# Natural key order in the sample's dilated mixture, and prompt heads prepared one head in front

## Chip, cores and metric

The kernel runs on one core of a Trainium2 chip. The metric is the device time of one execution in microseconds (us).

## What is computed

One hybrid encoder layer runs on two request groups with shared weights, a prompt of 512 tokens and a sample of 1024. Each group goes through an input layer norm, a token mixer, cross-attention into 256 memory tokens and a squared-ReLU MLP, with a layer norm behind each. The token mixer has eight heads of mixture a and eight of mixture b, 64 wide. Mixture a adds up three banded attentions, each with its own softmax, weighted by their log-sum-exp; b is a two-dimensional neighbourhood attention. What matters here is the pattern of a:

```
DILATED_PATTERNS = ((128, 1), (512, 4), (2048, 16))
def dilated_window_attention(q, k, v, window, dilation):
    # Query t attends to keys t + dilation*j, |j| <= (window/2)/dilation
    ...
    s = jnp.einsum('bdnqhc,bdnkhc->bdnhqk', qb, kb) * (hd ** -0.5)
    s = jnp.where(valid, s, NEG_INF)
    p = jnp.exp(s - m)
```

## The kernel before

All products are made from fp32r operands that are split in a high and a low part. A head's queries lie as one stack of 64 rows high and 64 rows low (qs), its keys as two stacks, k1 (high over low) and k2 (low over high), so that a score block is two matmuls, qs with k1 and qs with k2 (L502, L503).

Prompt heads of mixture a use one dense block of 512 keys per 128 queries. For the sample the three patterns are done in two kinds of units, four units a head. Units 1 and 2 (`attn_a1`, L579, first loop) are the local pattern: for each block of 128 queries, the up to 256 keys around it. Units 3 and 4 (second loop) are the dilated patterns: the tokens are split in four residue classes modulo 4, and each class of 256 queries meets its class of 256 keys, two blocks of 128 queries per class. A unit holds four blocks, so a head makes 16 score matmuls of each kind. The values of the dilated units are made by transposing every fourth column (L457); those of the local units by transposing adjacent columns (L409).

Before the change, the sample's keys lie in residue order over all 1024 tokens: all tokens of class 0, then 1, 2 and 3. For this, `stack` (L352) first copies 512 projected and rotated tokens, high part on ACT (L359) and low part on GpSimd (L360), into a buffer pair in residue order. The pair is `env["perm"]`, taken once from the tag "gb" (L650), so all 16 stacks of the sample use the same one. Eight DMAs on SP's queue (L366 to L370) then lay out the head: two natural query halves from the projection's buffers (hd<-qt) and six from the copies (hd<-gb), the residue queries and both key stacks, each row in four runs of 128 columns. A dilated unit then reads one run of keys, and a local unit reads four runs; its scores come out in residue order, and the masked maximum (L482) reads the mask and writes the probabilities with a step of four, so that the probabilities are natural again.

A head's attention (`unit`, L470) is a generator of four steps: scores, mask, maximum and exponentials; transposes of the probabilities and their split; products with v; transposing back. `push` (L566) adds a unit and lets each unit in flight take its next step; then it runs one entry of the mixer's `fill` list, if any. The plan holds 16 prompt heads and then 16 sample heads, a before b, in pairs that share weights and values; each has its preparation (weights, projections, `stack`, values, bias) and its units (one for a prompt head; four and two for sample heads of a and b). `attend` (L710) walks through them and spreads the preparation of later heads over the pushes of the present one. `lead(j)` says beside which head the preparation of head j stands: prompt heads stand two in front, sample heads one. Before that walk, head 0, the input norm of sample tile 8, head 1 and the input norms of tiles 9 to 11 are traced (L924). An input norm (`ln_in`, L220) loads 128 tokens, normalises them on VectorE, ACT and GpSimd (`layer_norm`, L148), stores them and transposes them eight times. Its gain and bias take two of the eight buffers of the tag "tok". A pair of prompt heads takes four of these eight: three for queries and keys, one for values.

The traced order is a priority: a scheduler takes what is ready by its own clock and gives out buffers as they come free, so engines need not follow the order of the source.

Of the kernel before, what the change touches and what calls it, by code (L numbers as in the profile page):

```python
# [31 lines left out]
def f32(ap):  # L32
    return ap.bitcast(F32)
# [3 lines left out]
def tile_encoder_layer(ctx: ExitStack, tc: tile.TileContext, d, outs):  # L37
# [232 lines left out]
    def mixer(r, fill):  # L270
# [80 lines left out]

        def stack(hd, sh, sl, g):  # L352

            qs, k1, k2 = hd[0:3]
            tt = slice(g * 512, (g + 1) * 512)
            kh, kl = sh, sl
            if r:
                kh, kl = env["perm"]
                A.activation(residues(kh), by_residue(f32(sh)), AF.Copy)  # L359
                G.tensor_copy(residues(kl), by_residue(f32(sl)))  # L360
                kh, kl = residues(kh), residues(kl)
                k1, k2, qp = (residues(k)[:, :, g * P:(g + 1) * P] for k in hd[1:4])
            else:
                k1, k2 = k1[:, tt], k2[:, tt]
            for o, x, y, z in ((slice(0, 64), sh, kh, kl), (slice(64, P), sl, kl, kh)):
                S.dma_start(f32(qs[o, tt]), f32(x[0:P:2]))  # L366
                if r:
                    S.dma_start(f32(qp[o]), f32(y[0:P:2]))
                S.dma_start(f32(k1[o]), f32(y[1:P:2]))
                S.dma_start(f32(k2[o]), f32(z[1:P:2]))  # L370

        def head_tile(is_b):
            t = act.tile([P, 4096], F32R, name="hd", tag="act")
# [93 lines left out]
                last = vt  # L467
                yield

        def unit(hd, v, h, blocks, norm=None, then=None, scale=1.0, local=False):  # L470

            qs, k1, k2 = hd[0:3]
            order, keyed = (by_residue, residues) if local else (lambda a: a, lambda a: a)
            st = sb.tile([P, 16], F32, name="st", bufs=4)
            probs, todo = [], []
            s, sx, pr, x = None, 512, None, 512

            def soften():  # L480
                for i, so, p, bias in todo:
                    V.tensor_tensor_reduce(out=order(p), in0=keyed(so), in1=order(bias), scale=1.0, scalar=LOWEST, op0=ALU.add,  # L482
                                           op1=ALU.max, accum_out=st[:, 8 + i:9 + i])
                    nm, den = st[:, 2 * i + 1:2 * i + 2], st[:, 2 * i:2 * i + 1]
                    V.tensor_scalar(nm, st[:, 8 + i:9 + i], -scale, None, op0=ALU.mult)  # L485
                    A.activation(p, p, AF.Exp, bias=nm, scale=scale, accum_out=den)  # L486
                todo.clear()
# [91 lines left out]
        def attn_a1(hd, v, h, tab, hg):  # L579
            for j in range(2):  # L580
                bl = []
                for b in range(4 * j, 4 * j + 4):
                    lead, n = (64, 192) if b == 0 else (0, 192) if b == 7 else (0, 256)
                    k0 = (b * P - 64 + lead) // 4
                    bl.append((cols(b * P, P), lambda z, k0=k0, n=n: residues(z)[:, :, k0:k0 + n // 4],
                               tab[:, lead:lead + n], n, lead, 256, (b, (b + 1) % 8)))

                def then(raw, j=j):
                    S.dma_start(oas[0][j * 512:(j + 1) * 512, hg].rearrange("(i p) c -> p i c", p=P), raw)
                push(unit(hd, v, h, bl, then=then, local=True))  # L590
                yield
            for j in range(2):
                bl = []
                for q in (2 * j, 2 * j + 1):
                    for i in range(2):
                        bl.append((cols(q * 256 + i * P, P), cols(q * 256, 256),
                                   tab[:, 384 - P * i:640 - P * i], 256, 0, 256, (8 + 2 * q, 9 + 2 * q)))

                def then(raw, j=j):
                    for i in range(2):  # L600
                        S.dma_start(oas[1].rearrange("(h p q) g c -> q p h g c", p=P, q=4)[2 * j + i, :, :, hg],
                                    raw[:, 2 * i:2 * i + 2])
                push(unit((hd[3],) + hd[1:3], v, h, bl, then=then))
                yield
# [102 lines left out]

        return [x for is_b in (False, True) for pair in range(4) for x in pair_ab(pair, is_b)]

    def attend(heads, lead, after=()):  # L710

        for k, (_, units, n) in enumerate(heads):
            work = [f for j in range(len(heads)) if lead(j) == k for f in heads[j][0]]
            if k == len(heads) - 1:
                work += after
            us, done = units(), 0
            for i in range(n):
                next(us)
                while done < len(work) * (i + 1) // n:
                    work[done]()  # L720
                    done += 1
            for _ in us:
                pass
# [9 lines left out]
    def merge(t):  # L733
# [15 lines left out]
        for i in range(2):  # L749
# [2 lines left out]
        V.tensor_add(o, o, t[1][:, :, 0:64])  # L752
        S.dma_start(os_[1][rows, 0:512].rearrange("p (g c) -> p g c", g=8), o)

    plan = mixer(0, []) + mixer(1, [None] * 36 + [call(merge, t) for t in range(8)] +
                                [call(tok_load, 0, t) for t in range(4)])


# [162 lines left out]
            for f in extra.get((h, 1), ()):  # L921
                f()

    for f in plan[0][0] + [call(ln_in, 8)] + plan[1][0] + [call(ln_in, i) for i in range(9, 12)]:  # L924
        f()
    attend(plan, lambda j: j - 2 if j < 16 else j - 1, [call(y_tile, 0, t) for t in range(4)])
    while pipe:
        step()
    w_out_half(0, 0)
# [348 lines left out]
```

## Time and profile before

| | us |
|---|---|
| median of 3 runs (lowest, highest) | 2386.12 (2379.81, 2386.31) |
| the profiled execution | 2380.81 |
| its span, first to last instruction | 2379.0 |
| TensorE matmul busy | 2284.5 |
| VectorE busy | 1608.6 |
| ScalarE (ACT) busy | 1022.7 |
| GpSimd (POOL) busy | 879.3 |

The profile is of one execution. PE is TensorE's matmuls, PEld its weight loads, which overlap them; DVE is VectorE; SP issues DMAs. A name such as hd<-gb says what is written and what is read; L-numbers are lines of the kernel. A wait row says which instruction stood idle and what it was released by.

### The profile page before, as it was taken

What the parts mean: (1) busy time and instruction counts of PE and PEld (TensorE: products, weight loads), DVE (VectorE), ACT (ScalarE), POOL (GpSimd) and SP (SyncE); (2) the same over time, 40 slices, a digit from 0 to 9 for tenths busy, and PEclk for the clock granted to TensorE, in tenths of its full rate; (3) what the DMA queues carried; (4) which work ended last, traced back from release to release, by engine and by line L of the source; (5) the groups of instructions that cost most, each with busy time, mean ns of one, the idle gap of its engine ahead of it and who ended that gap; (6) DMA issues with size and microseconds to landing.
All of it is one profiled execution on the core that took longest, in us unless ns stands there. A gap on an engine that the chain in (4) does not pass through costs nothing. (4 is left out here: it accounts for less than half of the span.)

```text
span 2379.0 us, 33108 instructions
## 1 busy us (share of the span) xinstructions
PE 2284.5 (96%) x11124; PEld 1892.7 (80%) x11124; DVE 1608.6 (68%) x3297; ACT 1022.7 (43%) x2176; POOL 879.3 (37%) x820
## 2 busy tenths in 40 slices
PE   8989998999999999999999999999999999999997
PEld 6868777888888787777878877878888888887875
DVE  6265635677656667668676487767776696689786
ACT  4345645666555532334333333333354322344541
POOL 7564443223324211433154355555541314310221
PEclk9999999999999999999999999999999999999998
DMA  9675345677535642435335444344489999974781
GB/s 318 201 228 146 78 117 121 137 137 150 116 95 135 180 124 92 133 115 176 117 107 185 121 155 147 120 139 147 149 223 221 210 222 250 224 177 156 165 206 68
DMA packets 410235, 375.21 MB, mean 158 GB/s; under 512 B 72513, under 2 KB 326481, under 8 KB 410065
## 3 DMA queue, kind: packets, MB, share of 16 engines
q1 hardware_dynamic: 367056, 339.54, 49.7%
q0 software_dynamic: 43008, 33.56, 10.1%
q8 instruction: 88, 1.44, 0.3%
q14 instruction: 83, 0.67, 0.1%
HBM read 290.76 MB, written 52.98 MB: 144 GB/s over the span
## 5 line engine op out<-in xcount | busy, mean ns | idle before, releaser
L107 POOL TENSOR_TENSOR wl<-wraw,wh 128x512 fp32r<-128x512 f32 x80 | 106.2, 1344 | 218.5 <-ACT wh L106 169.3
L1062 ACT ACTIVATE wh<-q 128x512 fp32r<-128x512 f32 x176 | 110.1, 626 | 140.5 <-DMA q<-in_w_up_dram 61.5
L486 ACT ACTIVATE q<-q,st 128x256 f32<-128x256 f32 (+3 forms) x256 | 138.4, 544 | 60.3 <-DVE st L485 59.0
L1063 DVE TENSOR_TENSOR wh<-q,wh 128x512 fp32r<-128x512 f32 x176 | 125.8, 717 | 54.2 <-ACT wh L1062 53.9
L321 POOL TENSOR_TENSOR wl<-wraw,wh 128x256 fp32r<-128x256 f32 x128 | 94.0, 757 | 160.3 <-ACT wh L320 144.9
L1047 POOL DMA_DIRECT2D q<-in_w_up_dram x64 | 83.3, 1416 | 181.0 <-DVE h L1100 72.8
L532 DVE TENSOR_TENSOR pt<-t,pt 128x512 fp32r<-128x512 f32 x160 | 105.2, 670 | 54.8 <-ACT pt L531 54.0
L1047 POOL DMA_DIRECT2D q<-in_w_down_dram x64 | 56.4, 921 | 218.9 <-DVE wraw L1134 92.9
L1000 POOL TENSOR_TENSOR wl<-pt,wh 128x512 fp32r<-128x512 f32 x64 | 91.6, 1451 | 118.6 <-ACT wh L999 118.4
L544 PE MATMUL o<-pt,tok 128*128 128x256 f32 (+3 forms) x576 | 116.1, 315 | 9.1 <-ACT q L550 8.6
L531 ACT ACTIVATE pt<-t 128x512 fp32r<-128x512 f32 x160 | 89.6, 579 | 80.1 <-PE o L544 76.4
L107 POOL TENSOR_TENSOR wl<-qt,wh 128x512 fp32r<-128x512 f32 x64 | 101.6, 1608 | 51.3 <-ACT wh L106 43.4
L1013 DVE TENSOR_TENSOR tok<-tok,t 128x512 f32<-128x512 f32 x124 | 82.9, 680 | 37.5 <-PE t L131 37.4
L1013 DVE TENSOR_TENSOR tok<-tok,s 128x512 f32<-128x512 f32 x124 | 83.8, 679 | 29.7 <-PE s L131 29.4
L131 PE MATMUL pj<-x20h,wl 128*128 128x512 f32 x256 | 101.4, 396 | 2.5 <-POOL wl L107 2.3
L119 POOL TENSOR_TENSOR wl<-wraw,wh 128x512 fp32r<-128x512 f32 x48 | 64.7, 1366 | 103.7 <-ACT wh L118 103.7
L129 PE MATMUL pj<-x20h,wh 128*128 128x512 f32 x256 | 100.6, 393 | 1.0 <-ACT wh L106 0.9
L528 PE MATMUL t<-ident,q 128*128 128x128 f32 x624 | 97.9, 276 | 3.3 <-ACT q L486 1.8
L158 POOL TENSOR_TENSOR lnst<-lnst,mhalf 128x1 f32<-128x1 f32 x44 | 54.2, 1234 | 124.7 <-DVE lnst L157 124.6
L130 PE MATMUL pj<-x20l,wh 128*128 128x512 f32 x256 | 100.2, 391 | 0.0
L544 PEld LDWEIGHTS o<-pt,tok 128*128 128x128 f32 x576 | 85.0, 192 | 16.5 <-ACT q L550 11.3
L999 ACT ACTIVATE wh<-pt 128x512 fp32r<-128x512 f32 x64 | 36.9, 624 | 121.7 <-PE s L131 103.2
(497 smaller groups left out, 7527.9 us busy)
## 6 DMA issues: line engine op xcount, KB each, us to landing
q<-in_w_up_dram SPq DMA_DIRECT2D x128, 256.0 KB
q<-in_w_down_dram SPq DMA_DIRECT2D x128, 256.0 KB
wraw<-in_w_in_dram SPq DMA_DIRECT2D x96, 256.0 KB
qt<-in_w_up_dram SPq DMA_DIRECT2D x32, 512.0 KB
pt<-in_w_down_dram SPq DMA_DIRECT2D x32, 512.0 KB
q<-in_w_up_dram POOLq DMA_DIRECT2D x64, 256.0 KB, 8.1
q<-in_w_down_dram POOLq DMA_DIRECT2D x64, 256.0 KB, 5.9
sa<-kv SPq DMA_DIRECT2D x28, 512.0 KB
```

The lines of the kernel that those rows point to most:

```text
L107: G.tensor_sub(wl[:, sl], r, f32(wh[:, sl]))
L129: T.matmul(out, lh[k], rh[k], start=(k == 0), stop=False, skip_group_check=True)
L130: T.matmul(out, lh[k], rl[k], start=False, stop=False, skip_group_check=True)
L131: T.matmul(out, ll[k], rh[k], start=False, stop=(k == n - 1), skip_group_check=True)
L486: A.activation(p, p, AF.Exp, bias=nm, scale=scale, accum_out=den)
L528: T.transpose(t[:, x:x + P], p, ident)
L532: V.tensor_sub(lo[:, 0:x], t[:, 0:x], f32(hi[:, 0:x]))
L544: T.matmul(o[:, q0:q0 + n], v(c, h), part[:, x:x + n], start=(done == 0 and part is hi), stop=(done == total - 1 and part is lo), skip_gro ...
L1013: V.tensor_add(x, x, q)
L1047: G.dma_start(out, src, accum_op=ADD)
L1062: A.activation(dst[0], x, AF.Copy)
L1063: low.tensor_sub(dst[1], x, f32(dst[0]))
```

## The change

In `stack` the keys go to their places in natural order, straight from the projection's buffers; only the queries for the dilated units come from the residue copy, in residue order within each 512 tokens. The local units read plain runs, and the masked maximum has no reordering any more. The dilated units take their queries from `512 * i + q * 128` and their keys as every fourth column. `lead` goes: every head is prepared one head in front, and the input norms of sample tiles 8 to 11 move into the prompt's `fill` list, beside its heads 1 to 4.

```diff
         def stack(hd, sh, sl, g):
             qs, k1, k2 = hd[0:3]
             tt = slice(g * 512, (g + 1) * 512)
-            kh, kl = sh, sl
+            ph, pl = env["perm"] or (None, None)
             if r:
-                kh, kl = env["perm"]
-                A.activation(residues(kh), by_residue(f32(sh)), AF.Copy)
-                G.tensor_copy(residues(kl), by_residue(f32(sl)))
-                kh, kl = residues(kh), residues(kl)
-                k1, k2, qp = (residues(k)[:, :, g * P:(g + 1) * P] for k in hd[1:4])
-            else:
-                k1, k2 = k1[:, tt], k2[:, tt]
-            for o, x, y, z in ((slice(0, 64), sh, kh, kl), (slice(64, P), sl, kl, kh)):
+                A.activation(residues(ph), by_residue(f32(sh)), AF.Copy)
+                G.tensor_copy(residues(pl), by_residue(f32(sl)))
+            for o, x, w, y in ((slice(0, 64), sh, sl, ph), (slice(64, P), sl, sh, pl)):
                 S.dma_start(f32(qs[o, tt]), f32(x[0:P:2]))
+                S.dma_start(f32(k1[o, tt]), f32(x[1:P:2]))
+                S.dma_start(f32(k2[o, tt]), f32(w[1:P:2]))
                 if r:
-                    S.dma_start(f32(qp[o]), f32(y[0:P:2]))
-                S.dma_start(f32(k1[o]), f32(y[1:P:2]))
-                S.dma_start(f32(k2[o]), f32(z[1:P:2]))
+                    S.dma_start(f32(hd[3][o, tt]), f32(y[0:P:2]))
...
-        def unit(hd, v, h, blocks, norm=None, then=None, scale=1.0, local=False):
+        def unit(hd, v, h, blocks, norm=None, then=None, scale=1.0):
...
-            order, keyed = (by_residue, residues) if local else (lambda a: a, lambda a: a)
...
-                    V.tensor_tensor_reduce(out=order(p), in0=keyed(so), in1=order(bias), scale=1.0, scalar=LOWEST, op0=ALU.add,
+                    V.tensor_tensor_reduce(out=p, in0=so, in1=bias, scale=1.0, scalar=LOWEST, op0=ALU.add,
...
-                    k0 = (b * P - 64 + lead) // 4
-                    bl.append((cols(b * P, P), lambda z, k0=k0, n=n: residues(z)[:, :, k0:k0 + n // 4],
-                               tab[:, lead:lead + n], n, lead, 256, (b, (b + 1) % 8)))
+                    bl.append((cols(b * P, P), cols(b * P - 64 + lead, n), tab[:, lead:lead + n], n, lead, 256,
+                               (b, (b + 1) % 8)))
...
-                push(unit(hd, v, h, bl, then=then, local=True))
+                push(unit(hd, v, h, bl, then=then))
...
-                        bl.append((cols(q * 256 + i * P, P), cols(q * 256, 256),
+                        bl.append((cols(512 * i + q * P, P), cols(q, 256, 4),
...
-    def attend(heads, lead, after=()):
+    def attend(heads, after=()):
         for k, (_, units, n) in enumerate(heads):
-            work = [f for j in range(len(heads)) if lead(j) == k for f in heads[j][0]]
-            if k == len(heads) - 1:
-                work += after
+            work = heads[k + 1][0] if k + 1 < len(heads) else after
...
-    plan = mixer(0, []) + mixer(1, ...)
+    plan = mixer(0, [None] + [call(ln_in, i) for i in range(8, 12)]) + mixer(1, ...)
...
-    for f in plan[0][0] + [call(ln_in, 8)] + plan[1][0] + [call(ln_in, i) for i in range(9, 12)]:
+    for f in plan[0][0]:
         f()
-    attend(plan, lambda j: j - 2 if j < 16 else j - 1, [call(y_tile, 0, t) for t in range(4)])
+    attend(plan, [call(y_tile, 0, t) for t in range(4)])
```

## Rows read from the trace of the kernel before

**Rows 1.** The page's part 1: busy us, share of the span, instructions.
```profile
PE 2284.5 (96%) x11124; PEld 1892.7 (80%) x11124; DVE 1608.6 (68%) x3297; ACT 1022.7 (43%) x2176; POOL 879.3 (37%) x820
```

**Rows 2.** Busy us by stretch (instructions), granted clock, DMA share, GB/s.
```profile
120.00:180.00 60.00, 50.49 (x230) 39.42 (x229) 41.58 (x80) 29.13 (x60) 36.65 (x32) 0.94 0.75 220
180.00:270.00 90.00, 88.91 (x442) 72.19 (x442) 47.01 (x120) 51.88 (x122) 35.69 (x42) 1.00 0.48 123
270.00:360.00 90.00, 83.25 (x474) 70.89 (x473) 46.72 (x170) 53.03 (x145) 47.41 (x78) 0.98 0.42 105
360.00:640.00 280.00, 263.32 (x1598) 230.71 (x1597) 185.26 (x608) 168.28 (x461) 79.47 (x104) 0.98 0.66 133
```

**Rows 3.** Waits of TensorE, 360 to 640 us: total us, times, longest us.
```profile
PE s L502 <- DMA hd<-gb: 9.3, 5, 5.6
PE o L544 <- ACT q L550: 4.9, 3, 1.9
PE t L528 <- ACT q L486: 1.6, 5, 0.6
```

**Rows 4.** Waits of ACT and GpSimd, 360 to 640 us.
```profile
ACT gb L359 <- DMA hd<-gb: 17.7, 8, 4.0
...
POOL gb L360 <- DMA hd<-gb: 38.3, 7, 7.8
```

**Rows 5.** Timeline of SP's queue, then TensorE's next row: start us, duration us.
```profile
368.11 0.49 SPq L366 DMA_DIRECT2D hd<-qt  x1
372.01 0.59 SPq L368 DMA_DIRECT2D hd<-gb  x1
...
376.25 0.61 SPq L369 DMA_DIRECT2D hd<-gb  x1
...
380.46 0.58 PE L502 MATMUL s<-hd 128*128 128x256 f32 x1 [5.61 <-DMA hd<-gb]
```

**Rows 6.** Lines L409 and L457: duration ns min/median/max, first and last start.
```profile
L409 PEld LDWEIGHTS pj<-ident,kv x96: 137/141/144, 127.6 to 802.8; 128*128 128x128 f32 x96
L409 PE MATMUL pj<-ident,kv x96: 271/273/329, 127.6 to 802.9; 128*128 128x128 f32 x96
...
L457 PEld LDWEIGHTS pj<-ident,kv x32: 196/210/213, 372.8 to 582.7; 128*128 128x128 f32 x32
L457 PE MATMUL pj<-ident,kv x32: 281/284/286, 372.9 to 582.8; 128*128 128x128 f32 x32
```

**Rows 7.** Timeline of TensorE: a local unit's scores, a dilated unit's scores, transposes.
```profile
388.03 0.28 PE L502 MATMUL s<-hd 128*128 128x256 f32 x1
...
388.15 0.28 PE L503 MATMUL s<-hd 128*128 128x256 f32 x1
...
390.70 0.28 PE L503 MATMUL s<-hd 128*128 128x256 f32 x1
390.82 0.28 PE L502 MATMUL s<-hd 128*128 128x256 f32 x1
...
391.06 0.60 PE L409 MATMUL pj<-ident,kv 128*128 128x128 f32 x4
391.50 0.64 PE L457 MATMUL pj<-ident,kv 128*128 128x128 f32 x4
```

**Rows 8.** Lines L359 (strided read) and L387 (adjacent) of ACT: duration ns min/median/max.
```profile
L359 ACT ACTIVATE gb<-qt x16: 1095/1132/1152, 361.8 to 614.5; 128x512 fp32r<-128x512 f32 x16
...
L387 ACT ACTIVATE qt<-qt x24: 616/632/633, 125.9 to 612.8; 128x512 fp32r<-128x512 f32 x24
```

**Rows 9.** Line L482, masked maximum: unit step (ANT_0) and step four (ANT_1), ns.
```profile
L482 DVE CUSTOM_DVE_ANT_0 q<-s,gb x96: 404/419/692, 139.4 to 642.8; 128x256 f32<-128x256 f32 x64, 128x512 f32<-128x512 f32 x32
...
L482 DVE CUSTOM_DVE_ANT_1 q<-s,gb x64: 492/622/664, 371.5 to 632.9; 128x256 f32<-128x256 f32 x48, 128x192 f32<-128x192 f32 x16
```

**Rows 10.** Waits of TensorE, 120 to 180 us.
```profile
PE pj L409 <- ACT kv L445: 2.7, 2, 2.0
PE t L137 <- POOL tok L173: 2.6, 2, 1.7
```

More of the change, by code (lines that the diff above doesn't have):

```diff
@@ L753, in merge @@
         S.dma_start(os_[1][rows, 0:512].rearrange("p (g c) -> p g c", g=8), o)
-    plan = mixer(0, []) + mixer(1, [None] * 36 + [call(merge, t) for t in range(8)] +
+    plan = mixer(0, [None] + [call(ln_in, i) for i in range(8, 12)]) + mixer(1, [None] * 36 + [call(merge, t) for t in range(8)] +
                                 [call(tok_load, 0, t) for t in range(4)])
```

## The prediction

> **What bounds the kernel now.** I read the page's busy shares first: TensorE is busy 96% of the span [rows 1], so time is lost or won in two ways only, by making TensorE's own work longer or shorter, or by closing a hole in it. Then the busy times by stretch [rows 2], cut where the stages lie: the first prompt heads with the last input norms (120 to 180 us), the other prompt heads of mixture a (to 270), prompt heads of b (to 360), the sample's mixture a (360 to 640). TensorE is idle 60 − 50.5 = 9.5 us, 1.1 us, 6.75 us and 280 − 263.3 = 16.7 us in them, 34 us in all, and everything that the change touches lies here. Next the waits of TensorE in the sample's mixture a [rows 3]: the largest is a score matmul that waits for the landing of key DMAs (hd<-gb), 9.3 us in five waits, one of them 5.6; then 4.9 us for ACT's eviction of the bank o. The waits of ACT and GpSimd in the same stretch [rows 4] show why keys are late: the residue copies (L359, L360) stand 17.7 and 38.3 us before the landing of hd<-gb. There is one buffer pair for the copies, and all six DMAs of a stack that read it must land before the next stack may write it. The DMA queue in order of time [rows 5] shows it once: the queries of a stack go out at 368.11, the first DMA that reads the copy only at 372.01, the last at 376.25, and TensorE starts again at 380.46.
>
> **Part 1: natural keys in the sample's mixture a.**
>
> *DMAs and copies.* Before, six of a stack's eight DMAs read the copies and write four runs of 128 columns per row; after, two do, the queries for the third and fourth unit of a head. The four key DMAs read sh and sl and can go right behind the first query DMA. Both copies stay, at 1.13 us on ACT [rows 8] and the like on GpSimd, 16 stacks each; they cost nothing new, and now only the two query DMAs wait for them. In the case of rows 5 the key DMAs gain 372.01 − 368.11 = 3.9 us. The 5.6 us wait should lose about 4, the other four (3.7 us together) about 2. ACT no longer sits before keys, so of the 4.9 us behind its evictions I count 1. Sum −7 us. At most 9.3 + 4.9 = 14 us could go; at the least nothing, if something else is late next. What is late next: the query copies, still behind the two query DMAs of the stack before, and on SP whatever is queued behind those two (the sample's weight loads and the stores of o). Nothing needs them before a head's third unit.
>
> *Softmax of the local pattern.* Its reduction reads mask and writes probabilities with a step of four now: 622 ns, against 404 with unit step [rows 9]; 64 of them become plain, 64 × 0.218 = 14 us of VectorE at most. VectorE is busy 185 of 280 us in this stretch [rows 2], so this is covered by TensorE's work; if the cover were gone it would be a gain. A unit gets 4 × 0.2 = 0.9 us shorter. Counted as zero.
>
> *Score matmuls of the local pattern.* Keys in four runs become one run. Four runs cost nothing now: starts are 120 ns apart (388.03, 388.15), as they are with one run (390.70, 390.82) [rows 7]. Zero.
>
> *Score matmuls of the dilated pattern.* Here is the price. Keys that lay in one run are now read with a step of four floats (16 bytes), as the moving operand: 8 heads × 2 units × 4 blocks × 2 = 128 matmuls of 128x256. No moving operand of the kernel before has such a step, so I bound it. Nothing above 118 to 120 ns per matmul is the lower end (a gain is excluded, since the same columns pass through). The nearest row is TensorE's own weight load with the very step: the transposes of L457 load weights from every fourth column in 210 ns, those of L409 in 141 ns from adjacent ones [rows 6], and four in a row fill (0.64 − 0.284)/3 = 119 ns each against (0.60 − 0.273)/3 = 109 [rows 7]. So the port delivers 128 strided columns in 119 ns, 0.93 ns a column, where 128 adjacent ones take 0.85. A moving operand is read faster than weights: 256 columns in 120 ns, 0.47 ns a column. If the strided rate is the port's limit of 0.93 ns, 256 columns take 238 ns, 118 more: 128 × 0.118 = 15 us. If only the surplus of the weight loads counts, 10 ns per 128 columns, it is 128 × 0.02 = 2.6 us. The upper end comes from ACT: a copy of 512 strided columns takes 1132 ns and one of adjacent columns 632 [rows 8], 0.98 ns more a column, which would be 250 ns a matmul and 32 us. I take 15 us, by the row of the same engine and step, and keep 0 and 32. TensorE has hardly a hole in this stretch, so it goes onto the path whole.
>
> These rows say that a step of 16 bytes costs weight loads 49% of their duration and ACT 79%. [...]
>
> **Part 2: prompt heads one in front, four input norms moved.** The prompt's heads 2 to 15 are prepared one head later, each with the same instructions, and head 14, beside which nothing was prepared, gets head 15. The four norms of the sample's second half go from before the first head to beside heads 1 to 4; with each go one load and one store on SP, VectorE's and ACT's passes, a power and a long addition on GpSimd, and eight transposes. Removed from 120 to 180 us: GpSimd and VectorE held TensorE up there, 2.7 us before v and 2.6 us before the norms' transposes [rows 10], 9.5 us idle with all others [rows 2]. Added: the norms' gain and bias keep two of the eight "tok" buffers until head 4, while a pair of prompt heads takes four, so a second pair can't be laid out until the first pair's scores are done. And a head's projections come one head nearer to its scores. At best the 9.5 us go, at worst as many come back in the next heads. The scheduler reorders what is ready, and the sample's heads, already one in front, leave TensorE 94% busy [rows 2]. I take zero, with ±9 kept for the range.
>
> **Sum.** +15 − 7 + 0 = +8 us. The profiled execution took 2380.81 us (span 2379.0), 5.3 us under the median of the three runs (2386.12; they lie from 2379.81 to 2386.31). I start from the middle of those two, 2383.5, and say **2391.5 us**, +0.3%, which is also about what a measurement of this kernel can tell from no change (7 us).
>
> **Rivals.**
> - *Strided keys are nearly free* (not slower). For it: the weight loads fill only 10 ns more per 128 columns. Against it: duration grew 69 ns, and the moving operand runs at twice their rate. 2.6 − 7 = −4.4 us: 2379; with the norms' 9.5 us regained too, 2370. It decides below some 55 ns more a matmul, where 128 of them equal the 7 us of waits.
> - *Strided keys at ACT's rate* (0.98 ns more a column): +32 − 7 = +25, 2408 us. Against it: TensorE's weight port is faster than that.
> - *The prompt stalls*: with six "tok" buffers in place of eight, pairs wait for each other, +9 us on top: 2400.
> - *The wait only changes its name*: the keys land earlier, but scores then wait for v or the query copies; −7 falls away, 2398.5.
>
> **How the numbers follow.** Forecast 0.40, strided keys free 0.30, ACT's rate 0.14, prompt stalls 0.08, wait renamed 0.08. The forecast's own spread (part 2) puts it slower at 0.24, within 0.3% at 0.15; the free case is faster at 0.19 and within at 0.10; the other three are slower but for 0.02. That makes faster 0.20, same 0.27, slower 0.53. The range takes the free case with part of the norms' gain, 2372, and reaches past ACT's rate with part of a prompt stall, 2416; what is left out are both extremes together.
>
> **What would show it.** Starts of the dilated score matmuls some 240 ns apart, the local ones still 120; the reduction of the local pattern near 404 ns; hd<-gb named before score matmuls for under 3 us, and the residue copies' waits shrunk; TensorE's idle time of 360 to 640 us near 10 us while the stretch is longer. The forecast is wrong if strided score matmuls stay under 175 ns apart, or if the prompt's stages end more than 9 us earlier or later than now.

## The result and the profile after

The change made the kernel faster: 2367.34 us (median of 4 runs, 2364.05 to 2368.47) against 2385.12 us of the kernel before (4 runs), a ratio of 0.9927, 95% interval 0.9909 to 0.9946. The forecast was 2391.5, with a range from 2372 to 2416. Medians here and below leave out the four executions (one of e1, one of e3, two of e5) that took far longer than the others of the same kernel. The profiled execution of the changed kernel took 2368.47 us with a span of 2366.7.

The page's busy row and its DMA row first, to hold against [rows 1]:

```profile
PE 2285.8 (97%) x11124; PEld 1895.9 (80%) x11124; DVE 1592.7 (67%) x3297; ACT 1024.2 (43%) x2176; POOL 884.6 (37%) x820
DMA packets 391803, 375.21 MB, mean 159 GB/s; under 512 B 72513, under 2 KB 301905, under 8 KB 391633
```

TensorE executes the same number of matmuls and is busy 1.3 us longer in all, while the span is 12.3 us shorter. Its idle time over the span went from 94.5 to 80.9 us, and the time in which it worked while the granted clock was at its lower level (0.50, against 1.00) from 29.4 to 18.0 us. About half of that time is lost: in the kernel before, projections of 128x512 start 0.43 us apart at 382 us, where the clock is low, and 0.23 us apart at 384 us, where it is not. Those two give 13.6 + 5.7 = 19.3 us, so TensorE's own work grew by some 7. (The DMA packets fell from 410235 by 18432, which is what the 16 stacks' six DMAs give that wrote four runs in each of 64 rows and write one now: 16 × 6 × 64 × 3.) The same stretches as in [rows 2], busy us of PE, PEld, DVE, ACT and POOL, granted clock, DMA share, GB/s:

```profile
120.00:180.00 60.00, 55.38 (x245) 45.02 (x244) 34.55 (x74) 28.53 (x63) 31.57 (x31) 0.91 0.70 192
180.00:270.00 90.00, 85.88 (x445) 69.64 (x444) 58.13 (x141) 56.47 (x128) 43.26 (x47) 1.00 0.51 147
270.00:360.00 90.00, 85.56 (x486) 73.08 (x485) 43.32 (x159) 52.97 (x144) 47.96 (x78) 1.00 0.42 108
360.00:640.00 280.00, 272.11 (x1598) 238.17 (x1598) 176.04 (x618) 168.14 (x456) 77.61 (x103) 0.99 0.56 132
```

TensorE's idle time is now 4.6, 4.1, 4.4 and 7.9 us, against 9.5, 1.1, 6.75 and 16.7. The last stretch lost the waits that the change is about. The waits of TensorE in it, to hold against [rows 3], then those of ACT and GpSimd [rows 4] (us in total, times, longest):

```profile
PE t L522 <- ACT q L480: 4.4, 4, 3.1
PE s L496 <- DVE st L476: 1.5, 3, 0.8
PE s L496 <- DMA hd<-qt: 0.9, 1, 0.9
...
ACT gb L359 <- DMA hd<-gb: 2.2, 1, 2.2
...
POOL gb L360 <- DMA hd<-gb: 13.3, 4, 5.5
```

No score matmul stands behind hd<-gb any more (9.3 us before), and the residue copies' own waits went from 17.7 to 2.2 and from 38.3 to 13.3 us. On SP's queue, to hold against [rows 5], the keys (L363, L364) go out right behind the queries, and only L366 reads the copy:

```profile
365.34 0.47 SPq L362 DMA_DIRECT2D hd<-qt  x1
365.87 0.59 SPq L363 DMA_DIRECT2D hd<-qt  x1
366.56 0.54 SPq L364 DMA_DIRECT2D hd<-qt  x1
367.19 1.73 SPq L366 DMA_DIRECT2D hd<-gb  x1
```

The price is there too. TensorE's timeline (start us, duration us), first scores of a local unit, then those of a dilated unit, to hold against [rows 7]:

```profile
377.88 0.28 PE L496 MATMUL s<-hd 128*128 128x256 f32 x1
378.00 0.28 PE L497 MATMUL s<-hd 128*128 128x256 f32 x1
...
381.50 0.42 PE L496 MATMUL s<-hd 128*128 128x256 f32 x1
381.74 0.41 PE L497 MATMUL s<-hd 128*128 128x256 f32 x1
381.97 0.41 PE L496 MATMUL s<-hd 128*128 128x256 f32 x1
382.20 0.42 PE L497 MATMUL s<-hd 128*128 128x256 f32 x1
```

Adjacent keys 120 ns apart, keys with a step of four (382.20 − 381.50)/3 = 233 ns. That is 113 ns more for each of 128 matmuls, 14.5 us.

Where the 12.3 us between the two profiled executions lie, the stages show. A stage is cut at TensorE's own instructions, here the first and last projection of the prompt's heads, the first product of the merged heads (y0h, the start of cross-attention), and the first projection of the MLP's input (x20h). Line, count, duration ns min/median/max, first and last start; the kernel before:

```profile
L129 PE MATMUL pj<-x0h,wh x192: 388/390/773, 113.6 to 347.4; 128*128 128x512 f32 x192
L816 PE MATMUL s<-wh,y0h x32: 388/390/497, 838.5 to 890.6; 128*128 128x512 f32 x32
L129 PE MATMUL pj<-x20h,wh x256: 387/390/501, 1376.0 to 1731.0; 128*128 128x512 f32 x128
```

and after:

```profile
L129 PE MATMUL pj<-x0h,wh x192: 387/389/776, 113.9 to 343.8; 128*128 128x512 f32 x192
L807 PE MATMUL s<-wh,y0h x32: 387/389/481, 834.3 to 886.8; 128*128 128x512 f32 x32
L129 PE MATMUL pj<-x20h,wh x256: 387/389/497, 1365.4 to 1718.2; 128*128 128x512 f32 x128
```

The prompt's stage ends 3.6 us earlier, cross-attention starts 4.2 us earlier, and it ends 10.6 us earlier: it is 531.1 us long in place of 537.6, though the diff touches nothing in it. The same cuts for every kernel that ran, in us of its profiled execution, with the cut between the sample's a and b at the first 128x384 score (the prompt's stage is counted to the end of its last projection):

| kernel | start | prompt | sample a | sample b | cross-att. | MLP, end |
|---|---|---|---|---|---|---|
| before | 113.6 | 234.7 | 297.6 | 192.6 | 537.6 | 1003.0 |
| after | 113.9 | 230.7 | 297.0 | 192.8 | 531.1 | 1001.3 |
| e0, the change again | 112.8 | 227.9 | 294.7 | 195.5 | 530.2 | 1001.9 |
| e1, natural keys alone | 112.8 | 239.6 | 293.5 | 195.1 | 539.5 | 1001.3 |
| e2, order alone | 113.3 | 229.7 | 290.0 | 195.4 | 530.3 | 1003.5 |
| e3, adjacent keys | 112.9 | 228.5 | 282.9 | 195.3 | 531.1 | 1002.8 |
| e4, one in front alone | 114.4 | 240.1 | 292.1 | 193.8 | 534.8 | 1002.4 |
| e5, norms alone | 113.7 | 238.2 | 294.1 | 195.3 | 532.7 | 1000.4 |
| e6, merges later | 114.0 | 239.9 | 300.8 | 195.1 | 532.8 | 1002.9 |
| e7, strided queries | 113.1 | 231.9 | 293.5 | 193.4 | 531.2 | 1001.3 |
| e8, sample's first head earlier | 113.9 | 235.4 | 292.8 | 194.0 | 538.0 | 1000.7 |
| e9, norms later | 111.5 | 236.1 | 297.1 | 194.6 | 531.4 | 1002.0 |

And of the sample's mixture a, from the same traces, how much of the stage TensorE stood idle, how long it worked at the lower level of the granted clock (0.50, against 1.00), and what is left when the idle time and half of that slow work are taken off, the stage's own work:

| kernel | keys | stage | idle | work at half clock | own work |
|---|---|---|---|---|---|
| before | residue | 297.6 | 16.7 | 6.3 | 277.7 |
| e2 | residue | 290.0 | 12.7 | 3.4 | 275.6 |
| e1 | strided | 293.5 | 5.0 | 0 | 288.5 |
| after | strided | 297.0 | 7.9 | 3.2 | 287.5 |
| e0 | strided | 294.7 | 7.7 | 0 | 287.0 |
| e3 | adjacent | 282.9 | 9.2 | 0 | 273.7 |
| e7 | adjacent, queries strided | 293.5 | 6.1 | 3.4 | 285.7 |

In the kernel before, the clock falls at 376.5 us, inside the 5.6 us hole of [rows 5], and rises at 383.4 us, so that 2.9 us of work behind the hole run at the lower level.

### The profile page after: what moved, and what is told of

It reads as the page before. It is cut to its first block, busy times and chain, and to the rows that moved or that the text cites. A ratio compares the mean times of both kernels' runs of the same rounds, so it can differ in the third digit from the quotient of the medians.

```text
span 2366.7 us, 33116 instructions
## 1 busy us (share of the span) xinstructions
PE 2285.8 (97%) x11124; PEld 1895.9 (80%) x11124; DVE 1592.7 (67%) x3297; ACT 1024.2 (43%) x2176; POOL 884.6 (37%) x820
## 5 line engine op out<-in xcount | busy, mean ns | idle before, releaser
L480 ACT ACTIVATE q<-q,st 128x256 f32<-128x256 f32 (+3 forms) x256 | 138.2, 543 | 62.2 <-DVE st L479 60.0
L321 POOL TENSOR_TENSOR wl<-wraw,wh 128x256 fp32r<-128x256 f32 x128 | 94.5, 762 | 146.4 <-ACT wh L320 119.9
L1038 POOL DMA_DIRECT2D q<-in_w_down_dram x64 | 56.2, 917 | 217.7 <-DVE wh L1054 112.8
L1004 DVE TENSOR_TENSOR tok<-tok,s 128x512 f32<-128x512 f32 x124 | 83.7, 678 | 29.6 <-PE s L131 29.4
L106 ACT ACTIVATE wh<-wraw 128x512 fp32r<-128x512 f32 x80 | 47.9, 627 | 103.4 <-PE pj L131 27.5
L522 PEld LDWEIGHTS t<-ident,q 128*128 128x128 f32 x624 | 74.4, 141 | 21.4 <-ACT q L480 9.1
```

The costliest lines, as they stand in the source:

```text
L522: T.transpose(t[:, x:x + P], p, ident)
L1004: V.tensor_add(x, x, q)
L1038: G.dma_start(out, src, accum_op=ADD)
```

## The experiments

A ratio is always to runs of the kernel before in the same session. Lines of a short diff are against the kernel before where nothing else is said. The first theory after the result was that the order of the work had won what the forecast put at zero; the rival was that the strided reads were nearly free and the natural keys had won it.

**e1, natural keys alone.** After's layout and units with before's order (against the changed kernel):

```diff
...
-            work = heads[k + 1][0] if k + 1 < len(heads) else after
+            work = [f for j in range(len(heads)) if lead(j) == k for f in heads[j][0]]
...
-    plan = mixer(0, [None] + [call(ln_in, i) for i in range(8, 12)]) + mixer(1, ...)
+    plan = mixer(0, []) + mixer(1, ...)
...
-    for f in plan[0][0]:
+    for f in plan[0][0] + [call(ln_in, 8)] + plan[1][0] + [call(ln_in, i) for i in range(9, 12)]:
...
```

> The first half of the change alone: natural keys, with the prompt heads two in front and the four norms in front of the first head, as in the kernel before. Theory A (the key path pays): the holes of the sample's mixture a close, 17 us idle there go to about 8 and its slow-clock stretches go, against 14 to 15 us for the strided reads; all of the change's gain of some 18 us stands here or in what follows, 2367 to 2372 us. Theory B (the order of the prompt pays): the natural keys are a wash, 2381 to 2388 us, with the prompt's end (last projection from x0) at 348 us as before. Theory C (the scheduler's new order of the later stages pays): the time hangs on the length of cross-attention from the first w_out product to the MLP, 537.6 us before and 531.1 after, whichever half is in.

Measured 2380.9 us, ratio 1.0008 [0.9999, 1.0017]: no change. In the trace the sample's mixture a gets 297.6 − 293.5 = 4.1 us shorter. Its row of that stretch:

```profile
360.00:640.00 280.00, 275.01 (x1633) 242.43 (x1632) 180.11 (x626) 171.99 (x467) 80.81 (x106) 1.00 0.57 134
```

Idle time is 5.0 us and the granted clock 1.00 throughout, against 16.7 us and 0.98. Own work grew by 10.8 us, idle time shrank by 11.7, and 6.3 us of work at half clock (3.1 us of loss) went. The whole time shows nothing of the 4.1 us: in this profile the prompt took 4.9 us longer than in that of the kernel before, with the same list of TensorE's instructions, and cross-attention 1.9. So price and gain of the natural keys nearly cancel.

**e2, the order alone.** Before's layout and units, with after's `attend`, fill list and start.

```diff
-    def attend(heads, lead, after=()):
+    def attend(heads, after=()):
...
-            work = [f for j in range(len(heads)) if lead(j) == k for f in heads[j][0]]
+            work = heads[k + 1][0] if k + 1 < len(heads) else after
...
-    plan = mixer(0, []) + mixer(1, ...)
+    plan = mixer(0, [None] + [call(ln_in, i) for i in range(8, 12)]) + mixer(1, ...)
...
-    for f in plan[0][0] + [call(ln_in, 8)] + plan[1][0] + [call(ln_in, i) for i in range(9, 12)]:
+    for f in plan[0][0]:
...
```

> The second half alone: every head one in front and the four norms beside prompt heads 1 to 4, with the keys in residue order as before. Theory A: 2381 to 2388 us, the sample's mixture a keeps its 17 us of holes. Theory B: the prompt ends near 344.5 us in place of 348.2, and since no strided read is paid the kernel is at 2367 or under, down to 2360 us. Theory C: the cross-attention takes about 531 us, so some 2375 us with the prompt's 4 us.

Measured 2364.03 us, ratio 0.9933 [0.9919, 0.9947], as much as the whole change. Against the kernel before its stages differ by −0.3, −5.0, −7.6, +2.8, −7.3 and +0.5 us, −16.9 in all. So the gain is the order's, and in these two traces it comes at three places, only one of which is the prompt; sample b gives 2.8 us back.

**e3, adjacent keys.** The changed kernel with the dilated units reading 256 adjacent keys. It leaves out the choice of every fourth key, so that its scores are of other keys than the layer's:

```diff
-                        bl.append((cols(512 * i + q * P, P), cols(q, 256, 4),
+                        bl.append((cols(512 * i + q * P, P), cols(q * 256, 256),
```

> The changed kernel, but the dilated units read 256 adjacent keys in place of every fourth one (the scores are then of other keys than the reference's). The order of every engine's instructions is that of the changed kernel, so the difference is the price of the step alone. If a strided key matmul costs 113 ns more, as its starts 233 ns apart in the changed kernel's trace say, 128 of them are 14.5 us: 2353 us. If the holes of the stage absorb part of it, 2355 to 2362; if the slower matmuls are covered, 2367.

Measured 2357.2 us, ratio 0.9907 [0.9891, 0.9924]. Every engine has the same list of instructions in the same order as in the changed kernel, so this is the step of four by itself: the scores start 0.11 to 0.12 us apart, and sample a takes 282.9 us against 297.0, 14.1 us less, where 128 × 0.113 gives 14.5. The whole time shows less of it, 0.20% to 0.37% below the change's two ratios (5 to 9 us), with intervals of about ±0.15% on each. Part of the 14.1 us is chance: the profile of e3 is of its fastest execution and that of the changed kernel of its slowest; against e0's profile, also of its fastest, sample a is 11.8 us shorter. The rows say that the step is paid in full; the medians agree in sign and not closely in size.

**e4 and e5, each half of the order alone.** One head in front with the four norms still ahead of the first head, and the norms beside heads 1 to 4 with the prompt's heads still two in front:

```diff
-    def attend(heads, lead, after=()):
+    def attend(heads, after=()):
...
-            work = [f for j in range(len(heads)) if lead(j) == k for f in heads[j][0]]
...
+            work = heads[k + 1][0] if k + 1 < len(heads) else after
...
-    for f in plan[0][0] + [call(ln_in, 8)] + plan[1][0] + [call(ln_in, i) for i in range(9, 12)]:
+    for f in plan[0][0] + [call(ln_in, i) for i in range(8, 12)]:
...
```

```diff
-    plan = mixer(0, []) + mixer(1, ...)
+    plan = mixer(0, [None] + [call(ln_in, i) for i in range(8, 12)]) + mixer(1, ...)
...
-    for f in plan[0][0] + [call(ln_in, 8)] + plan[1][0] + [call(ln_in, i) for i in range(9, 12)]:
+    for f in plan[0][0] + plan[1][0]:
```

> The kernel before with prompt heads prepared one in front, but the four norms still in front of the first head. If the lead is what pays and the norms' place is nothing: as fast as the second half alone, some 0.67% under before, 2363 us on the chip of the first runs. If both must go together (norms beside the heads alone gave nothing): within 0.3% of before, with the prompt's stage at 235 us or more in place of 230. If the cross-attention's new order is half of the gain: it comes with 537 us or 531 us there, whichever order the scheduler makes, and the total moves with it by 6 us.

> The kernel before with one thing changed: the four input norms of the sample's second half stand beside prompt heads 1 to 4, with the heads still prepared two in front and the keys in residue order. Theory B in its narrow form (it is the burst of norms in front of the first head that hurts): the idle time of 120 to 180 us falls from 9.5 to under 5 us and the kernel takes about 2377 to 2381. If the lead is what counts: 2385. Theory C: about 2379, by the cross-attention's 531 us.

Measured 2379.05 us, 0.9986 [0.9977, 0.9996], for e4, and 2380.6 us, 1.0003 [0.9991, 1.0014], for e5. Neither half carries the gain. The windows of e4:

```profile
120.00:180.00 60.00, 50.52 (x234) 39.73 (x233) 39.84 (x73) 29.70 (x60) 39.51 (x34) 0.94 0.70 211
180.00:270.00 90.00, 86.14 (x425) 68.39 (x424) 50.13 (x126) 51.38 (x118) 32.63 (x39) 1.00 0.53 130
270.00:360.00 90.00, 85.50 (x474) 72.12 (x473) 45.13 (x158) 54.39 (x147) 47.31 (x80) 0.96 0.39 98
```

and of e5:

```profile
120.00:180.00 60.00, 53.94 (x247) 43.01 (x246) 30.78 (x68) 28.16 (x66) 30.95 (x32) 0.97 0.67 191
180.00:270.00 90.00, 82.51 (x411) 65.92 (x411) 56.70 (x132) 51.98 (x116) 40.69 (x41) 0.98 0.48 142
270.00:360.00 90.00, 83.27 (x463) 70.47 (x462) 43.26 (x156) 51.36 (x140) 47.09 (x78) 0.98 0.41 102
```

With the norms in front, the first 60 us stay as idle as they were (9.5 us). With the norms moved and two heads in front that hole shrinks to 6.1 us, and 7.5 us of idle time come up behind it, where the kernel before had 1.1. Over 240 us TensorE is idle 17.8 and 20.3 us, 17.4 before; with both halves it is 15.3 (e2) and 13.2 (after). That the halves need each other is shown; why is shown only in part (at e8 below: the lead alone closes the hole at the start of the sample's mixture a, the norms' place alone does not). In e4 TensorE's longest waits from 120 to 260 us are still for the norms in front (transposes behind GpSimd, 3.0 us); in e5, from 170 to 260 us, they are projections that wait for VectorE (qt L385, 3.0 us). The forecast's "tok" buffers, which norms and pairs of heads share, would fit e5: on SP's queue a DMA that fills one stands 6.0 us behind a score there (L369), where none in before stands behind TensorE for more than 0.5 us. But no run changed them alone.

**e0, e6 and e7, in one session.** e0 is the changed kernel once more, as the measure for the others. e6 asks about cross-attention: it is the kernel before with the merges of the sample's heads two steps later, and nothing of the change in it.

```diff
-    plan = mixer(0, []) + mixer(1, [None] * 36 + [call(merge, t) for t in range(8)] +
+    plan = mixer(0, []) + mixer(1, [None] * 38 + [call(merge, t) for t in range(8)] +
```

e7 is the changed kernel with the roles swapped: the residue copy serves the keys, the queries are read with the step of four, as TensorE's weights, and the keys come as two adjacent runs of 128.

```diff
...
-                        bl.append((cols(512 * i + q * P, P), cols(q, 256, 4),
+                        bl.append((cols(512 * i + q, P, 4), lambda z, q=q: z.rearrange("p (g c x) -> p c g x", g=2, c=4)[:, q],
...
```

> The changed kernel itself, beside the others on one chip, so that the difference between it and its variants is not one between two sessions. All theories: 0.7% under the kernel before, as measured first.

> The kernel before with the merges of the sample's mixture a started two pushes later and nothing else. TensorE's order is that of before up to its 3047th row of 9318, so through the prompt and the sample's mixture a, and that of the changed kernel in the last 6128 rows, which hold the cross-attention and the MLP. If the cross-attention's gain is only the scheduler's other order there: that stage takes 531 us in place of 537.6, and the kernel is 0.2 to 0.3% under before with an unchanged prompt. If it needs the prompt's one-in-front order, the stage stays at 537 and the kernel at before's time.

> The changed kernel with the step moved from the moving to the stationary operand: the dilated units take their queries as every fourth column of the natural stack (weight loads) and their keys from the residue copy, in two adjacent runs of 128; the swapped high and low stack is one of the queries, so the head tile keeps its size and each stack its eight DMAs. Same result. If a strided weight load costs some 10 ns and a strided moving operand 113 ns, it is 13 us under the changed kernel in the trace's sample stage (283 to 285 us in place of 297), and 0.4 to 0.6% under it in time. If the price of the strided keys is absorbed elsewhere, as the single run with adjacent keys (0.2% under the change, across sessions) may say: 0 to 0.2%. If strided fp32r weights cost as much as strided keys: nothing.

e0: 2368.11 us, 0.9944 [0.9931, 0.9956]; the gain repeats. e6: 2380.38 us, 0.9994 [0.9981, 1.0007]; its cross-attention, from 849.9 to 1382.6 us in these rows, is 532.7 us long, as in the changed kernel and not as in the kernel before:

```profile
L816 PE MATMUL s<-wh,y0h x32: 387/389/481, 849.9 to 903.0; 128*128 128x512 f32 x32
...
L129 PE MATMUL pj<-x20h,wh x256: 387/389/500, 1382.6 to 1737.9; 128*128 128x512 f32 x128
```

The order of TensorE's instructions tells why the stage could change. Before and e8 share one order of their last 6692 instructions in the profile, out of 11124, which is all of the stage but its first hundred, and take 537.6 and 538.0 us; after, e0, e2, e3, e5, e6 and e7 share another (their last 6688) and take 530.2 to 532.8. (The expectations count in a shorter list, of 9318 rows.) e1, e4 and e9 have orders of their own in the stage and take 539.5, 534.8 and 531.4. The scheduler, which takes what is ready by its own clock, put a later stage in another order; that it did so because earlier ones ended otherwise is argued. The kernel before stands still around 900 us, behind the first products (columns as in [rows 2]):

```profile
900.00:910.00 10.00, 6.32 (x27) 4.40 (x26) 10.00 (x24) 0.60 (x1) 4.17 (x4) 0.95 0.11 34
910.00:920.00 10.00, 9.85 (x45) 8.63 (x45) 7.44 (x12) 3.75 (x7) 1.50 (x2) 0.71 0.39 137
```

and the changed kernel in two smaller pieces, the first of them earlier in the stage:

```profile
880.00:890.00 10.00, 7.87 (x38) 5.91 (x37) 8.38 (x21) 3.23 (x6) 1.29 (x2) 1.00 0.28 97
...
900.00:910.00 10.00, 8.94 (x49) 7.14 (x48) 10.00 (x18) 4.34 (x7) 2.90 (x2) 1.00 0.08 27
910.00:920.00 10.00, 10.00 (x56) 8.46 (x55) 9.08 (x14) 4.72 (x8) 0.00 (x0) 1.00 0.56 186
```

In the old order 3.7 us of idle time fall together, and the clock stands at its lower level from 909.0 to 915.8 us behind them; in the new one it is 2.1 and 1.1 us, and the clock doesn't fall. Over the whole stage the idle time is 20.8 and 21.0 us in the two kernels of the old order and 16.5 to 19.1 in the seven of the new, and the time at the lower level 6.8 us in both against 0 to 3.4. Part of the gain goes back in the stage before: sample b and cross-attention together take 731.1 us in the mean of the two and 726.0 in that of the seven, 5 us less. No whole time shows these 5 us by themselves: e6 and e5 have the new order without the gain of the prompt, and lie at 0.9994 and 1.0003. e6's interval allows 4.5 us of gain, and its profiled execution was its slowest run, with sample a at 300.8 us; e5's allows 2. So the 5 us rest on the stages of nine traces, not on a median.

e7: 2367.64 us, 0.9942 [0.9929, 0.9956], the change's own time. I had taken a strided weight load to be cheap by [rows 6]. It isn't for these matmuls (PEld is the weight load):

```profile
378.64 0.33 PEld L500 LDWEIGHTS s<-hd 128*128 128x128 f32 x1
378.77 0.40 PE L500 MATMUL s<-hd 128*128 128x256 f32 x1
378.87 0.33 PEld L499 LDWEIGHTS s<-hd 128*128 128x128 f32 x1
379.01 0.40 PE L499 MATMUL s<-hd 128*128 128x256 f32 x1
379.24 0.40 PE L500 MATMUL s<-hd 128*128 128x256 f32 x1
```

A load takes 330 ns where adjacent ones take 188, and the starts are 230 to 240 ns apart, as with strided keys.

**e8, the sample's first head one head earlier.** It asks whether the 5.6 us hole of [rows 5] is a matter of when that head is prepared.

```diff
-    attend(plan, lambda j: j - 2 if j < 16 else j - 1, [call(y_tile, 0, t) for t in range(4)])
+    attend(plan, lambda j: j - 2 if j < 17 else j - 1, [call(y_tile, 0, t) for t in range(4)])
```

> The kernel before, with the first sample head prepared one head earlier, beside prompt head 14, where nothing was prepared; keys, norms and the other heads as before. TensorE's order is before's for its first 1232 rows and its last 6126. If the hole of 5.4 to 5.6 us at the start of the sample's mixture a, and the slow clock that follows it in three profiles, come from this head's late preparation: the hole falls to about 2 us and the stage from 298 to 301 us to about 291, 0.25 to 0.4% of the whole, with the prompt and the cross-attention as before. If the hole comes from the residue copy of the keys alone (DMAs that wait for the copy), it stays over 4 us and the time is before's.

Measured 2378.23 us, 0.9988 [0.9977, 1.0000]. The waits for hd<-gb go on, with the longest down from 5.6 to 3.2 us:

```profile
PE s L502 <- DMA hd<-gb: 7.4, 5, 3.2
```

Sample a takes 292.8 us against 297.6. So the hole is partly a matter of that time. In e2, whose copies and key DMAs are those of the kernel before, the same wait is down to:

```profile
PE s L502 <- DMA hd<-gb: 2.9, 2, 1.6
```

What closes the hole there stands in TensorE's list of instructions. The scores that wait 5.6 us in the kernel before are the seventh to twelfth of the first sample head, and start 10.2 us behind its first. In e2 24 projections from x2 stand in front of them (the first, the last, and what follows):

```profile
368.82 0.50 PE L129 MATMUL pj<-x2h,wh 128*128 128x512 f32 x1 [0.69 <-DVE tok L411]
...
374.17 0.39 PE L131 MATMUL pj<-x2h,wl 128*128 128x512 f32 x1
374.40 0.38 PE L528 MATMUL t<-ident,q 128*128 128x128 f32 x2
374.54 0.36 PE L502 MATMUL s<-hd 128*128 128x256 f32 x1
```

In the kernel before, 24 such projections come right behind these scores, too late to fill the hole:

```profile
381.91 0.63 PE L129 MATMUL pj<-x2h,wh 128*128 128x512 f32 x1
```

In e2 the seventh score starts 8.2 us behind the first, hardly sooner, but TensorE has 5.6 us of other work meanwhile. All twelve traces agree: in after, e0, e2, e3, e4 and e7 the projections stand in front, and the seventh score waits for nothing; in the others they don't, and it waits 5.6 us (before), 5.4 (e5), 5.5 (e6), 3.2 (e8), 1.5 (e1) and 2.9 (e9). e4 has only the lead changed, so preparing the heads one in front is enough to put them there; in e9, which prepares them so too, the norms' later place undoes it. e1 and e9, whose keys are natural, wait less, and for DMAs that need no copy (hd<-qt).

**e9, norms later.** The changed kernel with the four norms beside heads 9 to 12:

```diff
-    plan = mixer(0, [None] + [call(ln_in, i) for i in range(8, 12)]) + mixer(1, ...)
+    plan = mixer(0, [None] * 9 + [call(ln_in, i) for i in range(8, 12)]) + mixer(1, ...)
```

> The changed kernel with the four norms beside prompt heads 9 to 12 (mixture b) in place of 1 to 4. If the gain of the prompt stage (229 us in five profiles of the new order, 238 in three of the old) comes from taking the burst of norms away from the first heads, the stage stays at 228 to 231 us. If the two tok buffers that gain and bias keep meanwhile are what counts, pairs of heads wait for longer: 233 us or more, and the kernel 0.2% or more over the changed one. If the norms must sit beside dense projections of mixture a to be covered: likewise over 233, with holes at 280 to 340 us.

Measured 2375.61 us, 0.9981 [0.9968, 0.9993]: by the medians two thirds of the gain or more are lost, only by where in the prompt the norms stand. Its prompt stage takes 236.1 us, with this row behind the first heads:

```profile
180.00:270.00 90.00, 83.12 (x398) 66.86 (x399) 47.32 (x120) 47.73 (x112) 34.19 (x43) 0.94 0.49 123
```

6.9 us idle there and a clock of 0.94, against 4.1 and 1.00 after. So it isn't enough to take the norms away from the first head, which was to give 228 to 231 us. The theory that norms need dense projections beside them expected holes at 280 to 340 us; the 4.0 us idle from 270 to 360 us, against 4.4 after, don't show them. The one of the "tok" buffers has its number, but nothing here shows its mechanism. Part of the loss lies elsewhere: the first sample head's scores wait again, as said above, and sample a is at 297.1 us.

## Why the prediction was wrong

**The price of strided keys: the number right, the way to it in part luck.** 118 ns were predicted and 113 measured; 15 us and 14.5. The row chosen out of a range from 0 to 32 us gave the right figure: 233/256 = 0.91 ns a column of the moving operand, where the strided weight load of [rows 6] gave 0.93. But the step behind it, that both operands are read at one strided rate, doesn't hold: in e7 the strided weight load of a score matmul takes 330 ns and the starts lie 235 ns apart, 1.84 ns a column of the weights and not 0.93. So the two figures met by luck. ACT's rate (250 ns more a matmul) and the free step both fall with the 233 ns measured against 120.

**The waits: right in kind, too small.** I took −7 us, with 14 the most. Alone (e1) the natural keys took 11.7 us of idle time out of the stage, and 6.3 us of work at half clock, worth 3.1 more, which I had not priced: the clock stood in [rows 2] (0.98) and in no term of the sum. So part 1 came out at −4.1 us in the stage's trace and at 1.0008 in the whole time, some 2 us, in place of +8. With the new order there was less left to cure (e2: 12.7 us idle, 3.4 us of work at half clock), and the natural keys cost 5 to 7 us of sample a there.

**The failed step: "I take zero, with ±9 kept for the range"** for part 2. The order alone gave 0.9933, some 16 us, outside the ±9. It acted at three places, of which I had priced one:
- The prompt. TensorE's list of instructions through this stage is the same in before, e1, e6 and e8, and they take 234.7, 239.6, 239.9 and 235.4 us, 237.4 in the mean; it is the same in after, e0, e2, e3 and e7, and they take 227.9 to 231.9, 229.7 in the mean. That is 7.7 us, near the "9.5 us" that I had named as the best case and not taken. I had allowed for the hole to come back behind; with both halves 3 us of it did (180 to 270 us: 4.1 us idle against 1.1), and with the norms moved alone 6.4 us. In part the gain is idle time (18.9 us in the mean of the one group, 13.9 in the other), in part the clock (12.8 us at the lower level in the mean, and 4.8). Which wait the two halves end together, and neither alone, stays open.
- The start of the sample's mixture a. The hole of 5.6 us [rows 5] closes without natural keys: 290.0 us in e2. With heads one in front (e2, e4), 24 projections stand in front of the scores that wait for keys, as shown at e8, and in e2 they start 0.23 us apart, the spacing of the higher clock; in the kernel before six scores and three projections run at the lower one behind the hole, these 0.43 us apart. So part 1 and part 2 had set out to win the same wait, and the forecast summed over them as if they had nothing in common. After the change a smaller hole stands there, 3.1 us behind ACT's exponentials (L480).
- Cross-attention, 5 us together with the stage before it, by a new order of the scheduler in a stage that the forecast called untouched ("everything that the change touches lies here"). This one rests on traces alone.

**The rivals.** "Strided keys are nearly free" named the sign and, with the norms' 9.5 us, 2370 us, near the measured time; that is luck, since its mechanism is wrong (113 ns are paid). "The prompt stalls" didn't happen with the whole change. "The wait only changes its name" did in small: ACT's exponentials and VectorE's maxima (4.4 and 1.5 us) are now the largest waits in the sample's mixture a.

**The signs I had named.** Score starts 240 ns apart and 120: seen, 233 and 120. hd<-gb below 3 us: gone. Idle time near 10 us "while the stretch is longer": 7.9, but the stretch isn't longer (297.0 us against 297.6). The prompt's stages "more than 9 us earlier" as a sign of a wrong forecast: they were 3.6 us earlier in the first pair of traces, their stage is 7.7 us shorter in the mean of nine, so this sign was set too far out to warn. The local units' maxima at unit step: all 160 instructions have the unit-step form now, with a median of 419 ns (the forecast's 404 ns is the least of a row of two shapes, not its median), and VectorE's busy time fell by 15.9 us [rows 1], which no stage of TensorE's shows as a gain of its own:

```profile
L476 DVE CUSTOM_DVE_ANT_0 q<-s,gb x160: 322/419/693, 136.2 to 637.2; 128x256 f32<-128x256 f32 x112, 128x512 f32<-128x512 f32 x32, 128x192 f32<-128x192 f32 x16
```

No version that computes all of the layer beats the change clearly: e2 and e7 stand level with it.

## What to carry to other kernels

A change in the order of a scheduled kernel is not worth zero because its parts are moved unchanged: ask which holes the new order can close, also holes that another part of the same change is meant to close, and expect later stages to be ordered anew. Look what stands in front of a waiting instruction on its engine: independent work moved there can close a hole as faster transfers can (24 projections closed that of 5.6 us in e2; natural keys alone left 1.5 us of it in e1). Compare TensorE's order of instructions stage by stage before looking for a cause in the code; two kernels with the same list in a stage measure the noise of that stage (227.9 to 231.9 us here). And price a strided read by a row of the same operand, engine and kind of matmul, since another row need not carry over: the step cost the transposes' weight loads 69 ns and those of the score matmuls 142.

## What the runs showed of the hardware

- A step of four floats costs a 128x256 fp32r score matmul 113 ns where the moving operand has it (233 ns apart, against 120), and 110 to 120 ns where the weights have it (230 to 240 ns apart; the load 330 ns against 188). The transposes' strided weight loads of the kernel before had risen only from 141 to 210 ns [rows 6], so they are no measure for those of the score matmuls (235/128 = 1.84 ns a column, against 0.93).
- Stretches at the lower level of the granted clock (0.50, against 1.00) differ between executions of the same list of instructions: 10.2 us of the prompt's stage in the profile of the changed kernel, none in e0's. The five profiles of the prompt's stage with that list lie from 227.9 to 231.9 us, so a stage time from one profile is good to some 4 us here.
